# A one-layer decoder step on one core: where the last scaling's inputs and the sums of the down weights are loaded and made

## The chip, the cores and the metric

The kernel runs on one core of one Trainium2 chip, as one program. Its engines are PE (TensorE, the matmuls, with its weight loads shown as PEld), DVE (VectorE), ACT (ScalarE), POOL (GpSimd) and SP (SyncE). All transfers of this kernel are issued from SP's queue, in the order in which they stand there. The metric is the time of one execution on the device in microseconds (us), lower being better.

## The reference

One decoder layer with D_MODEL 1024 is computed in fp32 for a prompt of 2048 tokens and for 8 samples of 8 tokens each, 2112 tokens in all:

```python
def decoder_layer(x, ...):
    h = rms_norm(x, lp['pre_mix_g'])
    z = jnp.einsum('bld,de->ble', h, lp['w_in'])
    ...  # window attention, spatial gating and memory attention, each with its own gate
    x = x + rms_norm(mixed, lp['post_mix_g'])
    f, new_conv = conv_ffn(rms_norm(x, lp['pre_ffn_g']), ...)
    x = x + rms_norm(f, lp['post_ffn_g'])

def conv_ffn(h, conv_past, w_up, conv_w, conv_b, w_down):
    up = jnp.einsum('bld,df->blf', h, w_up)            # 1024 -> 2*2816
    c = conv_b; c = c + ext[:, j:j + L] * conv_w[j]    # j = 0, 1, 2, along the tokens
    act = gelu(gate) * val
    return jnp.einsum('blf,fd->bld', act, w_down)      # 2816 -> 1024
```

The change touches the second half alone: the ConvFFN and the last line, which adds the scaled result f to x. In the kernel x after the first half is called x1.

## The kernel before, in words

**Products.** An fp32 matrix is split into a rounded part and a rest (`split`: ACT casts, line 76; DVE subtracts, line 77), and a product is made of three matmuls (`PASSES`). Tokens lie along the free dimension in three groups of 704 (T2), each of two halves of 352 (CW). Big products go by Strassen's scheme: a unit has 7 products (weights a11, s1, a12, s2, s4, s3, a22), each of 12 matmuls, and the last one, a22, is run behind the first one of the next unit. In a name such as `wa11_u0_8` the letters give the weight and u0_8 group 0, unit 8. Weights a11, a12 and a22 are loaded raw (`r0`, `r1`, `r3`, line 821) and split; the sums s1 to s4 (`ws`, line 847) are loaded ready made from DRAM (`sum_d`).

**Stages.** After the first stages (to about 1560 us) comes the up projection of the ConvFFN: 3 groups of 22 units, with the convolution, gelu and product of a unit on POOL, ACT and DVE beside the matmuls (`Sink`; lines 1140 to 1183). Then follows the down projection: in each group 8 quads by the same scheme (products added into 8 tiles `ys`, lines 1229 and 1234), and a plain part for the last six blocks of 128 features (line 1279, tiles `ps_p`).

**Work inside the up projection.** Three jobs beside the units themselves are issued between units by `jobs()`. (1) `prep_sums` makes the four sums of one block of down weights: it loads 4 raw blocks, makes 4 sums on DVE (line 113), splits and stores them; there are eight such preps, d0 to d7, after every fourth unit from u0_3 to u1_11. (2) `norms` makes the row factors `rb2` of the next group from a tile of sums of squares (8 small matmuls, line 88, DVE line 92, POOL line 95, 8 small matmuls, line 98, a copy, line 1087), for each half; it is issued after unit 14. (3) `operands` loads the 8 tiles of x1 for the next group and scales each by `rb2` on DVE (line 780), then makes sums and splits of them.

**The end of a group.** `final` makes the row factors `rs` (line 1301), scales the 8 tiles of f (line 1306), adds x1 (line 1310, tile `xf`, loaded at line 1304) and stores (line 1311). For groups 0 and 1 it is held back and issued inside the next group's first quad. The last group is cut in halves, so that only its second half stands behind the last matmul; of this one every other addition is on POOL.

**What sets the order.** The order of each engine's queue is set by a scheduler before the run. Tiles come from pools, and a tile of a pool is handed out as soon as its last user is done: `wof` holds the split or summed weights (11 buffers of 4096 bytes per partition), `rawf` the raw ones and the sums in the making (5 buffers), tag `ld` of `ldf` whole activation tiles (8 buffers), tag `x` of `sd` the x1 tiles of `final` (2 buffers), `yd` the results (10).

Of the kernel before, what the change touches and what calls it, by code (L numbers as in the profile page):

```python
# [9 lines left out]
F32 = mybir.dt.float32  # L10
# [5 lines left out]
P = 128  # L16
# [7 lines left out]
T2 = 704  # L24
CW = T2 // 2
NG2 = NTOK // T2
# [719 lines left out]
def stage2(tc, I, O, br, rbc_d, x1_d, acx_d, act_d, sum_d, sg_d, gains, split, PASSES, rstd_rows, prep_sums, m_d, acm_d):  # L746
# [148 lines left out]
    for phase in (gate_phase, mix_phase, ffn_phase):  # L895
        with ExitStack() as c2:
            for n, nm in (("ps2", "ps_"), ("ps3", "pst_")):
                env[n] = c2.enter_context(
                    tc.tile_pool(name=nm + phase.__name__, bufs=1, space=PSUM, reuse_waits="tile")
                )  # L900
            phase(c2, tc, env)
# [146 lines left out]
def ffn_phase(c2, tc, env):  # L1048

    pool = env["pool"]  # L1050
    env["lp"], env["rw"], env["wo"] = (
        pool(c2, nm, n, "right") for nm, n in (("ldf", 1), ("rawf", 5), ("wof", 11))
    )
    env["op_"] = {n: pool(c2, "f" + n, 4, "right") for n in ("b11", "t1")}
    env["op_"].update({n: pool(c2, "f" + n, 4) for n in ("b21", "t2", "b22", "t3", "t4")})
    for phase in (up_phase, down_phase):
        with ExitStack() as c3:
            phase(c3, tc, env)


def up_phase(c2, tc, env):

    nc, I, O, x1_d, acx_d, act_d, sum_d, gains, pool, ps2, Strassen, rstd_rows, prep_sums, m_d, acm_d = (
        env[n] for n in (
            "nc", "I", "O", "x1_d", "acx_d", "act_d", "sum_d", "gains", "pool", "ps2", "Strassen", "rstd_rows",
            "prep_sums", "m_d", "acm_d",
        )
    )
    op_, wo, rw, lp = (env[n] for n in ("op_", "wo", "rw", "lp"))
# [8 lines left out]
    def norms(src, nm):  # L1078

        rb = lp.tile([P, T2], F32, tag="rb", name=f"rb2_{nm}", bufs=1)  # L1080
        acc = lp.tile([P, T2], F32, tag="ld", name=f"acx_{nm}", bufs=8)
        nc.sync.dma_start(out=acc, in_=src)
        for c in range(2):
            psb = env["ps3"].tile([P, 512], F32, tag="st", name=f"ps_su{nm}_{c}", bufs=1)
            cols = slice(c * CW, (c + 1) * CW)
            rstd_rows(acc[:, cols], CW, psb[:, CW:], lambda c0, w: psb[:, c0 : c0 + w], lp, f"u{nm}_{c}")
            nc.vector.tensor_copy(out=rb[:, cols], in_=psb[:, :CW])
        return rb
# [11 lines left out]
    def late(o, rs):  # L1100

        g = NG2 - 1
        m = lp.tile([P, T2], F32, tag="ld", name=f"ml_{o}", bufs=8)
        nc.sync.dma_start(out=m, in_=m_d[o])
        x = lp.tile([P, T2], F32, tag="ld", name=f"xl_{o}", bufs=8)
        nc.sync.dma_start(out=x, in_=I["xT"][:, o, g * T2 : (g + 1) * T2])
        nc.vector.scalar_tensor_tensor(
            out=m, in0=m, scalar=gains[:, 2, o : o + 1], in1=rs, op0=ALU.mult, op1=ALU.mult
        )
        nc.vector.tensor_tensor(out=m, in0=m, in1=x, op=ALU.add)  # L1110
        nc.sync.dma_start(out=x1_d[g][o], in_=m)
        if o == 0:
            nc.scalar.activation(acx, m, AF.Square)
        else:
            nc.scalar.activation(x, m, AF.Square)
            nc.vector.tensor_tensor(out=acx, in0=acx, in1=x, op=ALU.add)
        if o + 1 == KT:
            nc.sync.dma_start(out=acx_d[g], in_=acx)
# [69 lines left out]
                nc.sync.dma_start(out=dst, in_=p)  # L1188

    def jobs():  # L1190
        ops, rs = ops0, None
        for g in range(NG2):
            for f in range(NF):
                yield f"u{g}_{f}", eng.weights(I["w3"][f], sum_d[f], False, f"u{g}_{f}"), ops, Sink(g, f)
                if f % 4 == 3 and 5 * g + f // 4 < 8:
                    i = 5 * g + f // 4
                    prep_sums(rw, wo, I["w4s"][i], sum_d[NF + 12 + i], f"d{i}")
                if g == 0 and 2 <= f < 2 + KT:
                    rs = rs or norms(acm_d, "m")
                    late(f - 2, rs)  # L1200
                if f == 14 and g + 1 < NG2:
                    rb = norms(acx_d[g + 1], str(g + 1))
            if g + 1 < NG2:
                ops = eng.operands(lambda k: x1_d[g + 1][k], f"u{g + 1}", 3, rb)

    eng.run(jobs())
    nc.sync.dma_start(out=O["ncv"], in_=ncv)


def down_phase(c2, tc, env):  # L1210
# [8 lines left out]
    op_, wo, rw, lp = (env[n] for n in ("op_", "wo", "rw", "lp"))  # L1219
    yp, sp = pool(c2, "yd", 10), pool(c2, "sd", 1)  # L1220
# [74 lines left out]
    def final(g, ys, acc, cs):  # L1295
        c0, c1 = cs[0] * CW, (cs[-1] + 1) * CW
        rs = sp.tile([P, T2], F32, tag="rs", name=f"rs_d{g}_{c0}")
        for c in cs:
            psb = env["ps3"].tile([P, 512], F32, tag="st", name=f"ps_sd{g}_{c}", bufs=1)
            rstd_rows(chunk(acc, c), CW, psb[:, CW:], lambda o0, w: psb[:, o0 : o0 + w], sp, f"d{g}_{c}")  # L1300
            nc.vector.tensor_copy(out=chunk(rs, c), in_=psb[:, :CW])
        for o in range(KT):
            x = sp.tile([P, T2], F32, tag="x", name=f"xf_{g}_{o}_{c0}", bufs=2)
            nc.sync.dma_start(out=x[:, c0:c1], in_=x1_d[g][o][:, c0:c1])
            y = ys[o][:, c0:c1]
            nc.vector.scalar_tensor_tensor(  # L1306
                out=y, in0=y, scalar=gains[:, 4, o : o + 1], in1=rs[:, c0:c1], op0=ALU.mult, op1=ALU.mult
            )
            e = nc.gpsimd if o % 2 and g + 1 == NG2 and cs[-1] else nc.vector
            e.tensor_tensor(out=y, in0=y, in1=x[:, c0:c1], op=ALU.add)  # L1310
            nc.sync.dma_start(out=O["yT"][:, o, g * T2 + c0 : g * T2 + c1], in_=y)

    end = held = None
    for g in range(NG2):
        ys = []
        for b in range(NB):
            ops = eng.operands(lambda k: act_d[8 * b + k][:, g * T2 : (g + 1) * T2], f"d{g}_{b}", None, None)
            for op in range(4):
                if b == 0:
                    ys += [yp.tile([P, T2], F32, tag="y", name=f"y_{g}_{2 * op + h}") for h in range(2)]  # L1320
                i, nm = 4 * b + op, f"d{g}_{b}_{op}"
                ws = eng.weights(I["w4s"][i], sum_d[NF + 12 + i], False, nm)
                end = quad(nm, ws, ops, ys[2 * op : 2 * op + 2], b == 0, end)
                if held:
                    final(*held)
                    held = None
        acts = load_acts(g)
        acc = sp.tile([P, T2], F32, tag="acc", name=f"acc_{g}")
        if g + 1 < NG2:
            plain(g, acts, ys, (0, 1), acc, end)  # L1330
            held, end = (g, ys, acc, (0, 1)), None
        else:
            plain(g, acts, ys, (0,), acc, end)
            plain(g, acts, ys, (1,), acc, lambda: final(g, ys, acc, (0,)))
            final(g, ys, acc, (1,))
# [135 lines left out]
```

## Time and profile before

| | |
|---|---|
| time, median of 3 runs | 3004.3 us (3001.31 to 3009.29) |
| the profiled execution's own time | 3005.72 us |
| its span, first to last instruction | 3003.9 us |
| PE busy | 2876.0 us (96%) |
| DVE, ACT, POOL busy | 69%, 47%, 16% |
| granted TensorE clock, mean over the span | 0.977 |

Of the page's parts, the line of busy shares says which engine could be the bound, and the slices show where that engine is not at nine tenths. The queries that follow from it are the waits of that engine by stretch, the timeline where it waits, and windows of its busy time with the clock it was granted. In a timeline row the bracket at the end is the idle time of the engine before the instruction, and what ended it.

### The profile page before, as it was taken

How to read it: one execution, taken by the hardware profiler on the slowest of the kernel's cores; microseconds unless marked ns; L12 is line 12 of the kernel's file. 1: busy time of each engine (PE TensorE's matmuls, PEld its weight loads, DVE VectorE, ACT ScalarE, POOL GpSimd, SP SyncE). 2: the span in 40 equal slices, each digit the busy share in tenths (PEclk: the TensorE clock that was granted, in tenths of full speed). 3: DMA queues.
4: the chain of work that ended last, by engine and by line, in shares of the span. 5: the costliest groups of instructions: out<-in, count | busy, mean ns of one | idle time of the engine just before them, and what ended most of it. 6: DMA issues, size and time to landing. Idle time of an engine off the chain costs nothing. (4 is left out here: it accounts for less than half of the span.)

```text
span 3003.9 us, 52626 instructions
## 1 busy us (share of the span) xinstructions
PE 2876.0 (96%) x19340; PEld 2829.2 (94%) x19340; DVE 2064.8 (69%) x3901; ACT 1397.5 (47%) x2799; POOL 488.3 (16%) x576
## 2 busy tenths in 40 slices
PE   8999999996999999999999899999999999999996
PEld 8998999996999999999989899999999999999996
DVE  6676567888867363478798677766775667667665
ACT  5555557333555353432235355644554454343332
POOL 3221100010000000035453121311231121000000
PEclk9999999998999999999999899999999999999998
DMA  6222224787989999867669788887777778576673
GB/s 209 53 69 85 76 68 126 258 303 248 328 296 371 332 356 346 320 212 264 212 249 364 291 304 310 319 288 278 246 277 247 240 238 279 196 273 223 233 246 119
DMA packets 310946, 732.33 MB, mean 244 GB/s; under 512 B 37968, under 2 KB 90192, under 8 KB 310672
## 3 DMA queue, kind: packets, MB, share of 16 engines
q1 hardware_dynamic: 310688, 728.97, 69.9%
q8 instruction: 153, 2.51, 0.3%
q14 instruction: 105, 0.86, 0.1%
HBM read 553.55 MB, written 176.27 MB: 243 GB/s over the span
## 5 line engine op out<-in xcount | busy, mean ns | idle before, releaser
L1023 PE MATMUL ps_p<-b,w_p 128*128 128x352 f32 x1728 | 287.2, 328 | 13.3 <-DVE m L1032 8.8
L1023 PEld LDWEIGHTS ps_p<-b,w_p 128*128 128x128 f32 x1728 | 283.3, 192 | 15.1 <-issue 10.2
L1165 DVE SCALAR_TENSOR_TENSOR c<-e,k_conv_w,c 128x704 f32<-128x704 f32 (+1 forms) x264 | 251.6, 954 | 43.3 <-ACT c L1161 36.0
L882 PE MATMUL ps_xu<-ot_u,ws_u 128*128 128x352 f32 x1584 | 274.9, 322 | 0.0
L882 PEld LDWEIGHTS ps_xu<-ot_u,ws_u 128*128 128x128 f32 x1584 | 257.1, 188 | 0.0
L1036 POOL TENSOR_TENSOR m<-m,sl 128x704 f32<-128x704 f32 x48 | 101.4, 2119 | 658.0 <-DVE sl L1035 651.8
L77 DVE TENSOR_TENSOR wa_u<-r_u,wa_u 128x512 fp32r<-128x512 f32 x198 | 138.6, 703 | 48.0 <-ACT wa_u L76 43.9
L1161 ACT ACTIVATE c<-e,k_conv_b,k_conv_w 128x704 f32<-128x704 f32 (+1 forms) x132 | 129.6, 981 | 78.6 <-DVE e L1140 43.5
L882 PE MATMUL ps_xu<-ob_u,wa_u 128*128 128x352 f32 x792 | 149.0, 325 | 9.7 <-ACT wa_u L76 9.7
L1152 POOL COPY tails<-e 128x2 f32<-128x2 f32 x88 | 79.2, 900 | 470.0 <-DVE e L1140 469.6
L882 PE MATMUL ps_xg<-ot_h,ws_g 128*128 128x352 f32 x864 | 151.1, 323 | 1.7 <-ACT ws_g L76 0.8
L882 PE MATMUL ps_wu<-ob_u,wa_u 128*128 128x352 f32 x792 | 147.0, 324 | 1.1 <-DVE ob_u L77 1.1
L882 PE MATMUL ps_yu<-ot_u,ws_u 128*128 128x352 f32 x792 | 143.2, 325 | 3.8 <-DVE sl L1035 2.2
L76 ACT CAST wa_u<-r_u 128x512 fp32r<-128x512 f32 x198 | 123.1, 623 | 47.1 <-PE ps_xu L882 15.7
L882 PEld LDWEIGHTS ps_xg<-ot_h,ws_g 128*128 128x128 f32 x864 | 140.6, 188 | 2.4 <-ACT ws_g L76 1.3
L882 PEld LDWEIGHTS ps_xu<-ob_u,wa_u 128*128 128x128 f32 x792 | 131.7, 190 | 9.9 <-ACT wa_u L76 9.9
L1279 PE MATMUL ps_p<-a,wd 128*128 128x352 f32 x864 | 140.1, 323 | 0.0
L1279 PEld LDWEIGHTS ps_p<-a,wd 128*128 128x128 f32 x864 | 138.4, 188 | 0.1
L882 PE MATMUL ps_xu<-ot_u,wa_u 128*128 128x352 f32 x792 | 138.0, 323 | 0.0
L882 PE MATMUL ps_yu<-ob_u,ws_u 128*128 128x352 f32 x792 | 137.7, 323 | 0.0
L882 PEld LDWEIGHTS ps_yu<-ot_u,ws_u 128*128 128x128 f32 x792 | 130.9, 190 | 4.6 <-DVE sl L1035 2.5
L1140 DVE TENSOR_TENSOR e<-p_u,ps_wu 128x352 f32<-128x352 f32 x66 | 34.3, 519 | 145.1 <-PE ps_wu L882 140.3
(381 smaller groups left out, 6786.2 us busy)
## 6 DMA issues: line engine op xcount, KB each, us to landing
ws_u<-sum_d SPq DMA_DIRECT2D x264, 512.0 KB, 4.9
r_u<-in_w_dram SPq DMA_DIRECT2D x286, 256.0 KB, 4.7
ws_g<-sum_d SPq DMA_DIRECT2D x96, 512.0 KB, 8.5
ws_d<-sum_d SPq DMA_DIRECT2D x96, 512.0 KB, 5.1
sum_d<-ws_u SPq DMA_DIRECT2D x88, 512.0 KB, 4.2
r_g<-in_wg_dram SPq DMA_DIRECT2D x120, 256.0 KB, 5.3
r_d<-in_w4s_dram SPq DMA_DIRECT2D x104, 256.0 KB, 4.4
sg_d<-sg SPq DMA_DIRECT2D x72, 352.0 KB, 5.0
```

The costliest lines, as they stand in the source:

```text
L76: nc.scalar.copy(out=hi, in_=src)
L77: nc.vector.tensor_tensor(out=lo, in0=src, in1=_f(hi), op=ALU.subtract)
L882: nc.tensor.matmul(ps[:, :CW], lhsT=ws[w][:, a, j], rhs=ops[o][j][:, b], start=(start and n == 0), stop=(n == 3 * HK - 1), skip_group_chec ...
L1023: nc.tensor.matmul(ps[:, c, :CW], lhsT=w[:, a, 4 * oo + k], rhs=bs[k][:, b, c * CW : (c + 1) * CW], start=(i == 0), stop=(i == 11),)
L1036: nc.gpsimd.tensor_tensor(out=mx[o], in0=mx[o], in1=sg, op=ALU.add)
L1140: lambda out, part: nc.vector.tensor_tensor(out=out, in0=part(p), in1=part(q), op=ALU.add), h, c
L1152: nc.gpsimd.tensor_copy(out=tails[:, ft], in_=e[:, T2 : T2 + 2])
L1161: nc.scalar.activation(c[:, :cwid], e[:, 2:ew], AF.Identity, bias=cb[:, ft : ft + 1], scale=cw[:, ft, 2:3])
L1165: nc.vector.scalar_tensor_tensor(out=c[:, :cwid], in0=e[:, t : t + cwid], scalar=cw[:, ft, t : t + 1], in1=c[:, :cwid], op0=ALU.mult, op1= ...
L1279: nc.tensor.matmul(ps[:, :CW], lhsT=w[k // 4][:, a, k % 4], rhs=acts[k][c][:, b], start=(n == 0), stop=(n == 3 * ND - 1),)
```

## The change

Four edits are made. The pool `wof` has 10 buffers instead of 11. The preps d0 to d7 are issued after units u0_11, u0_14, u1_2, u1_5, u1_8, u1_11, u1_14 and u2_2. `norms` is issued after unit 18 instead of 14. In `final` the x1 tiles come from 4 buffers instead of 2 for the first two groups, and for the last group from the 8 buffers of tag `ld`.

```diff
--- before.py
+++ after.py
@@ -1049,7 +1049,7 @@
 
     pool = env["pool"]
     env["lp"], env["rw"], env["wo"] = (
-        pool(c2, nm, n, "right") for nm, n in (("ldf", 1), ("rawf", 5), ("wof", 11))
+        pool(c2, nm, n, "right") for nm, n in (("ldf", 1), ("rawf", 5), ("wof", 10))
     )
     env["op_"] = {n: pool(c2, "f" + n, 4, "right") for n in ("b11", "t1")}
     env["op_"].update({n: pool(c2, "f" + n, 4) for n in ("b21", "t2", "b22", "t3", "t4")})
@@ -1188,17 +1188,18 @@
                 nc.sync.dma_start(out=dst, in_=p)
 
     def jobs():
+        preps = [(g, f) for g, fs in ((0, (11, 14)), (1, (2, 5, 8, 11, 14)), (2, (2,))) for f in fs]
         ops, rs = ops0, None
         for g in range(NG2):
             for f in range(NF):
                 yield f"u{g}_{f}", eng.weights(I["w3"][f], sum_d[f], False, f"u{g}_{f}"), ops, Sink(g, f)
-                if f % 4 == 3 and 5 * g + f // 4 < 8:
-                    i = 5 * g + f // 4
+                if (g, f) in preps:
+                    i = preps.index((g, f))
                     prep_sums(rw, wo, I["w4s"][i], sum_d[NF + 12 + i], f"d{i}")
                 if g == 0 and 2 <= f < 2 + KT:
                     rs = rs or norms(acm_d, "m")
                     late(f - 2, rs)
-                if f == 14 and g + 1 < NG2:
+                if f == 18 and g + 1 < NG2:
                     rb = norms(acx_d[g + 1], str(g + 1))
             if g + 1 < NG2:
                 ops = eng.operands(lambda k: x1_d[g + 1][k], f"u{g + 1}", 3, rb)
@@ -1300,7 +1301,10 @@
             rstd_rows(chunk(acc, c), CW, psb[:, CW:], lambda o0, w: psb[:, o0 : o0 + w], sp, f"d{g}_{c}")
             nc.vector.tensor_copy(out=chunk(rs, c), in_=psb[:, :CW])
         for o in range(KT):
-            x = sp.tile([P, T2], F32, tag="x", name=f"xf_{g}_{o}_{c0}", bufs=2)
+            if g + 1 == NG2:
+                x = lp.tile([P, T2], F32, tag="ld", name=f"xf_{g}_{o}_{c0}", bufs=8)
+            else:
+                x = sp.tile([P, T2], F32, tag="x", name=f"xf_{g}_{o}_{c0}", bufs=4)
             nc.sync.dma_start(out=x[:, c0:c1], in_=x1_d[g][o][:, c0:c1])
             y = ys[o][:, c0:c1]
             nc.vector.scalar_tensor_tensor(
```

**DVE, up projection, before.** The scaling of x1 for group 1 (`x_u1`, line 780) and what stands around it; `d1` is the second prep, `u0_8` the unit whose weights come next.

```order
L780 SCALAR_TENSOR_TENSOR x_u1_0_21183<-x_u1_0_21183,c_gains_164,rb2_1_20117 128x704
L780 SCALAR_TENSOR_TENSOR x_u1_1_21189<-x_u1_1_21189,c_gains_164,rb2_1_20117 128x704
L780 SCALAR_TENSOR_TENSOR x_u1_2_21195<-x_u1_2_21195,c_gains_164,rb2_1_20117 128x704
L780 SCALAR_TENSOR_TENSOR x_u1_3_21201<-x_u1_3_21201,c_gains_164,rb2_1_20117 128x704
L780 SCALAR_TENSOR_TENSOR x_u1_4_21227<-x_u1_4_21227,c_gains_164,rb2_1_20117 128x704
L780 SCALAR_TENSOR_TENSOR x_u1_5_21233<-x_u1_5_21233,c_gains_164,rb2_1_20117 128x704
L780 SCALAR_TENSOR_TENSOR x_u1_6_21239<-x_u1_6_21239,c_gains_164,rb2_1_20117 128x704
L790 TENSOR_TENSOR t_u1_0_21207<-x_u1_0_21183 128x352
L113 TENSOR_TENSOR s3_d1_19078<-r1_d1_19076,s2_d1_19070 128x512
L790 TENSOR_TENSOR t_u1_1_21212<-x_u1_1_21189 128x352
L780 SCALAR_TENSOR_TENSOR x_u1_7_21245<-x_u1_7_21245,c_gains_164,rb2_1_20117 128x704
L790 TENSOR_TENSOR t_u1_2_21217<-x_u1_2_21195 128x352
```

**DVE, up projection, after.** The same scaling in the changed kernel.

```order
L1087 COPY rb2_1_20641<-ps_su1_1_20657 128x352
L1140 TENSOR_TENSOR e0_0_19_20693<-p1_u0_19_20708,ps_wu0_19_20747 128x352
L1179 TENSOR_TENSOR c0_0_18_20622<-c0_0_18_20622,c1_0_18_20725 128x704
L780 SCALAR_TENSOR_TENSOR x_u1_0_21087<-x_u1_0_21087,c_gains_164,rb2_1_20641 128x704
L780 SCALAR_TENSOR_TENSOR x_u1_1_21093<-x_u1_1_21093,c_gains_164,rb2_1_20641 128x704
L780 SCALAR_TENSOR_TENSOR x_u1_2_21099<-x_u1_2_21099,c_gains_164,rb2_1_20641 128x704
L780 SCALAR_TENSOR_TENSOR x_u1_3_21105<-x_u1_3_21105,c_gains_164,rb2_1_20641 128x704
L780 SCALAR_TENSOR_TENSOR x_u1_4_21131<-x_u1_4_21131,c_gains_164,rb2_1_20641 128x704
L780 SCALAR_TENSOR_TENSOR x_u1_5_21137<-x_u1_5_21137,c_gains_164,rb2_1_20641 128x704
L780 SCALAR_TENSOR_TENSOR x_u1_6_21143<-x_u1_6_21143,c_gains_164,rb2_1_20641 128x704
L780 SCALAR_TENSOR_TENSOR x_u1_7_21149<-x_u1_7_21149,c_gains_164,rb2_1_20641 128x704
L77 TENSOR_TENSOR wa22_u0_20_20827<-r3_u0_20_20828,wa22_u0_20_20827 128x512
```

The sums of prep d1 stood on both sides of the eight scalings (its fourth sum `s3_d1` behind seven of them); now no row of a prep stands near them, and what follows is a weight of unit 20.

**SP, the end of the program, before.** The last 12 rows of transfers; `xf` are loads of x1, `out_yT` stores of the result.

```order
L1311 DMA out_yT_dram<-y_2_0_31363 128x352
L1311 DMA out_yT_dram<-y_2_2_31536 128x352
L1304 DMA xf_2_3_352_33150<-x1_d2_159 128x352
L1304 DMA xf_2_4_352_33155<-x1_d2_159 128x352
L1311 DMA out_yT_dram<-y_2_3_31537 128x352
L1311 DMA out_yT_dram<-y_2_4_31655 128x352
L1304 DMA xf_2_5_352_33160<-x1_d2_159 128x352
L1304 DMA xf_2_6_352_33165<-x1_d2_159 128x352
L1311 DMA out_yT_dram<-y_2_5_31656 128x352
L1311 DMA out_yT_dram<-y_2_6_31774 128x352
L1304 DMA xf_2_7_352_33170<-x1_d2_159 128x352
L1311 DMA out_yT_dram<-y_2_7_31775 128x352
```

**SP, the end of the program, after.** Twelve of its last 18 rows; the load of `xf_2_0_352` stands some rows above.

```order
L1308 DMA xf_2_1_352_33140<-x1_d2_159 128x352
L1315 DMA out_yT_dram<-y_2_6_31774 128x352
L1315 DMA out_yT_dram<-y_2_7_31775 128x352
L1308 DMA xf_2_2_352_33145<-x1_d2_159 128x352
L1308 DMA xf_2_3_352_33150<-x1_d2_159 128x352
L1308 DMA xf_2_4_352_33155<-x1_d2_159 128x352
L1308 DMA xf_2_5_352_33160<-x1_d2_159 128x352
L1308 DMA xf_2_6_352_33165<-x1_d2_159 128x352
L1308 DMA xf_2_7_352_33170<-x1_d2_159 128x352
L1315 DMA out_yT_dram<-y_2_1_31364 128x352
L1315 DMA out_yT_dram<-y_2_3_31537 128x352
L1315 DMA out_yT_dram<-y_2_5_31656 128x352
```

The loads stood between the stores, each pair behind the stores of an earlier pair; now all eight stand ahead of `y_2_1`, the first store of this half (the two stores above it are of the half before).

**DVE, first quads of group 1 in the down projection, before.** The last rows ahead of the scaling of group 0's result (line 1306), which is 8 rows long; its first two are shown.

```order
L77 TENSOR_TENSOR wa22_d1_0_2_29953<-r3_d1_0_2_29954,wa22_d1_0_2_29953 128x512
L77 TENSOR_TENSOR wa11_d1_0_3_30054<-r0_d1_0_3_30055,wa11_d1_0_3_30054 128x512
L1301 COPY rs_d0_0_29747<-ps_sd0_1_29761 128x352
L1306 SCALAR_TENSOR_TENSOR y_0_0_27986<-y_0_0_27986,c_gains_164,rs_d0_0_29747 128x704
L1306 SCALAR_TENSOR_TENSOR y_0_1_27987<-y_0_1_27987,c_gains_164,rs_d0_0_29747 128x704
```

**DVE, the same place after**, from the last two rows of that scaling on; the copy of `rs` now stands right behind `wa22_d1_0_2`.

```order
L1310 SCALAR_TENSOR_TENSOR y_0_6_28330<-y_0_6_28330,c_gains_164,rs_d0_0_29747 128x704
L1310 SCALAR_TENSOR_TENSOR y_0_7_28331<-y_0_7_28331,c_gains_164,rs_d0_0_29747 128x704
L77 TENSOR_TENSOR wa11_d1_0_3_30054<-r0_d1_0_3_30055,wa11_d1_0_3_30054 128x512
L1314 TENSOR_TENSOR y_0_0_27986<-y_0_0_27986,xf_0_0_0_29774 128x704
L1314 TENSOR_TENSOR y_0_1_27987<-y_0_1_27987,xf_0_1_0_29779 128x704
```

The rest of weight `wa11_d1_0_3` (line 77) stood ahead of the copy of `rs`; in the changed kernel it stands behind the scaling and ahead of the first addition of `xf`.

## Rows read from the trace of the kernel before

**Rows 1.** windows: busy us by engine, granted clock, DMA share, GB/s
```profile
1690.00:1700.00 10.00, 6.05 (x19) 5.58 (x20) 7.37 (x15) 2.28 (x4) 0.00 (x0) 0.50 0.77 243
1720.00:2100.00 380.00, 380.00 (x2385) 379.75 (x2385) 270.03 (x401) 202.15 (x363) 75.55 (x114) 1.00 0.85 299
2100.00:2480.00 380.00, 380.00 (x2375) 380.00 (x2374) 261.45 (x450) 195.40 (x358) 91.72 (x198) 1.00 0.74 248
```

**Rows 2.** PE's waits, 1540 to 1720 us: total us, times, longest
```profile
PE ps_xu L882 <- ACT wa_u L76: 9.7, 1, 9.7
...
PE ps_su L98 <- POOL rstd_u L95: 2.4, 1, 2.4
...
PE ps_yu L882 <- DMA ws_u<-sum_d: 1.7, 1, 1.7
```

**Rows 3.** timeline, 1676 to 1703 us: start, duration, instruction, idle before
```profile
1677.77 0.71 PE L88 MATMUL ps_su<-ones,acx 128*88 128x1 f32 x8
...
1683.90 6.12 DVE L780 SCALAR_TENSOR_TENSOR x_u<-x_u,c_gains,rb 128x704 f32<-128x704 f32 x7
...
1684.38 7.03 SPq L821 DMA_DIRECT2D r_u<-in_w_dram  x3
...
1691.09 0.62 ACT L76 CAST ws_d<-s_d 128x512 fp32r<-128x512 f32 x1 [10.01 <-DVE s_d L113]
...
1692.28 0.95 PE L882 MATMUL ps_xu<-ob_u,wa_u 128*128 128x352 f32 x2 [9.66 <-ACT wa_u L76]
...
1695.49 3.88 PE L882 MATMUL ps_yu<-ot_u,ws_u 128*128 128x352 f32 x12 [1.67 <-DMA ws_u<-sum_d]
...
1701.88 1.28 PE L882 MATMUL ps_wu<-ob_u,wa_u 128*128 128x352 f32 x7
```

**Rows 4.** timeline, 2094 to 2108 us, the scaling for the last group
```profile
2095.58 1.02 PE L98 MATMUL ps_su<-ident,rstd_u 88*128 88x88 f32 x8
...
2098.51 2.67 DVE L780 SCALAR_TENSOR_TENSOR x_u<-x_u,c_gains,rb 128x704 f32<-128x704 f32 x3
...
2098.88 2.08 PE L882 MATMUL ps_yu<-ob_u,ws_u 128*128 128x352 f32 x12
...
2100.80 1.92 PE L882 MATMUL ps_xu<-ob_u,wa_u 128*128 128x352 f32 x11
...
2101.70 4.39 DVE L780 SCALAR_TENSOR_TENSOR x_u<-x_u,c_gains,rb 128x704 f32<-128x704 f32 x5
```

**Rows 5.** page, DMA issues: KB each, median us to landing
```profile
ws_u<-sum_d SPq DMA_DIRECT2D x264, 512.0 KB, 4.9
```

**Rows 6.** waits of PE from 2480 us to the end
```profile
PE ps_xd L882 <- ACT y L1229: 17.5, 3, 6.8
```

**Rows 7.** timeline, 2662 to 2684 us, change of group in down
```profile
2667.48 6.99 DVE L1306 SCALAR_TENSOR_TENSOR y<-y,c_gains,rs_d 128x704 f32<-128x704 f32 x8
...
2677.86 0.45 ACT L1229 COPY y<-ps_xd 128x352 f32<-128x352 f32 x1 [5.77 <-DMA out_yT_dram<-y]
```

**Rows 8.** timeline, 2960 us to the end
```profile
2961.41 4.06 DVE L1306 SCALAR_TENSOR_TENSOR y<-y,c_gains,rs_d 128x352 f32<-128x352 f32 x8
...
2976.45 0.76 PE L88 MATMUL ps_sd<-ones,acc 128*88 128x1 f32 x8 [1.99 <-DVE acc L1293]
...
2978.13 0.15 DVE L92 TENSOR_SCALAR rstd_d<-ps_sd 88x4 f32<-88x4 f32 x1
...
2982.24 4.72 DVE L1306 SCALAR_TENSOR_TENSOR y<-y,c_gains,rs_d 128x352 f32<-128x352 f32 x8
...
2983.40 1.20 POOL L1310 TENSOR_TENSOR y<-y,xf 128x352 f32<-128x352 f32 x1 [3.82 <-DVE y L1306]
...
2986.89 1.11 DVE L1310 TENSOR_TENSOR y<-y,xf 128x352 f32<-128x352 f32 x2
...
3000.25 0.92 POOL L1310 TENSOR_TENSOR y<-y,xf 128x352 f32<-128x352 f32 x1 [3.44 <-DMA xf<-x_d]
...
3001.20 0.33 SPq L1311 DMA_DIRECT2D out_yT_dram<-y  x1
```

## The prediction

> **What bounds the kernel now.** I read the page's busy shares first: PE is busy for 2876.0 of 3003.9 us, so only the stretches where PE is not busy can be won, and anything else helps only by shortening one of them. Then the windows: from 1720 to 2480 us, most of the up projection, PE is busy for all of 380.00 and of 380.00 us at the full clock [rows 1], so nothing done beside it there costs time. Then the waits of PE on both sides of that stretch. Before it there are three that belong to one place: 9.7 us on a weight's cast, 2.4 us on POOL's rstd and 1.7 us on a load of sums [rows 2]. Behind it stand 17.5 us in three waits on the copies into y [rows 6]. Last, the timeline at those places and behind the last matmul: after 2976.45 us PE has only the small matmuls of the row factor left, and the end is set by the additions of x1, each of which waits for its load [rows 8].
>
> The first place, 1677.77 to 1701.88 us, reads as follows [rows 3]. Seven scalings of x_u1 stand on DVE from 1683.90 for 6.12 us, and the fourth sum of prep d1 is ordered behind them. SP, with the raw buffers taken by that prep, needs 7.03 us for three loads of weights. ACT idles 10.01 us for the sum, and only behind the sum's cast comes the cast that PE waits for, 9.66 us. So neither the burst nor the prep is the cause alone: the burst delays the prep, the prep holds ACT's order and the buffers, and PE pays.
>
> **The change, part by part.**
>
> *The preps and the norms.* What PE did from 1677.77 to 1701.88, 24.11 us, is 16 small matmuls and 2 + 2 + 12 + 10 = 26 big ones. At the full clock 12 big ones take 1.92 us (2098.88 to 2100.80), the small ones 0.71 and 1.02 us [rows 3, 4]. So the work is worth 26 x 0.16 + 1.73 = 5.9 us and the loss is 18.2 us. Of it 2.4 + 9.7 + 1.7 are waits; the rest is mostly the clock after them, granted at 0.50 from 1690 to 1700 us [rows 1], the lower of its two levels (1.2 GHz), at which 12 matmuls took 3.88 us [rows 3]. In the new order the scaling of x_u1 has no prep beside it, and the burst by itself cost PE nothing the other time it ran: 2.67 and 4.39 us of scaling for group 2 lie inside a stretch in which PE never stopped [rows 1, 4]. Six preps (d2 to d7) lay in that stretch as well, so a prep by itself also cost nothing. I take the whole 18.2 us as gained; it would be nearer 9 if a smaller collision comes in its place, and nothing if an equal one does. The wait of 2.4 us on rstd is in the 18.2: in the new order 29 matmuls stand between the two sets of small ones, 29 x 0.16 = 4.6 us of cover for a chain of that length.
>
> *Ten weight buffers instead of eleven.* A unit uses 7 of them in 7 x 1.92 = 13.44 us. With 11, a buffer can be handed out 10 products ahead of its use, 19.2 us; with 10, 17.3 us. A load of sums lands in 4.9 us [rows 5], so between preps nothing is late. A prep holds four of them for a while and leaves 5 products, 9.6 us, where it was 11.5. That still covers 4.9, but not 4.9 plus the 7.03 us that three issues took when the raw buffers were held [rows 3], which would be 2.3 us over, at worst at each of the preps. Bounds: 0, and 8 preps x about 1.2 us (half of them that late) = 9 us. The row nearest to it is the full 760 us of PE with six preps at 11.5 us [rows 1], so I take 2 us lost. A gain I exclude: fewer buffers start no load earlier.
>
> *The last scaling.* Before, two x1 tiles are loaded at a time; behind the scaling, which starts at 2982.24, the additions run at the pace of a load, a store and a wait, to 3000.25 + 0.92 us, and the span ends 2.7 us after the last store is issued at 3001.20 [rows 8]. After, all eight loads of the last half stand ahead of its first store, and their buffers are free when the additions of the half before are done, so they land before 2981 us. Two things follow. First, the row factor: DVE's line 92 started at 2978.13, though the small matmuls were done at 2976.45 + 0.76 = 2977.21; it stood behind an addition that waited for x1. With about 0.1 us of handing over that is 0.8 us earlier, and the scaling starts at 2981.4. Second, the additions. DVE needs at least 4.06 us for eight scalings without POOL beside them, and 4 x 0.55 us for its own additions, 6.3 us. With one POOL addition beside it the scaling took 4.72, or 0.66 more [rows 8]; four such make it 8.9 us. The last store is issued at most 0.4 us later. So the end lies between 2981.4 + 6.3 + 2.7 = 2990.4 and 2981.4 + 8.9 + 0.4 + 2.7 = 2993.4, a gain of 13.5 to 10.5 us. I take 11.5, nearer the lower one, since the only scaling with POOL beside it shows the stretch.
>
> The Trainium skill, page "SBUF — State Buffer", on the shared port pair, says more against this: a VectorE instruction with two SBUF inputs and a GpSimd instruction exclude each other, and the later one waits for the whole of the other. By that rule the four additions of POOL, 0.92 us each alone [rows 8], would add 3.7 us to DVE's 6.3, and the gain would be about 9.4 to 9.8 us. The trace agrees that there is a price, but shows 0.66 us of it for one addition rather than 0.92.
>
> *Four x1 tiles for groups 0 and 1.* PE's wait there is 6.8 us at its longest and ends with ACT's copy into y, which waited 5.77 us for the first store of the old result [rows 6, 7]. That store needs the eight scalings, 6.99 us [rows 7], and one addition; its two x1 tiles were there already. More tiles cannot start it earlier. In the new order one subtraction of 0.7 us (line 77) stands between the scaling and the first addition, and the scaling starts earlier by as much, where it stood before. I take 0 for both changes together, bounds 1.5 lost and 1.5 gained (one such subtraction each way, twice).
>
> *Sum.* 3005.7 (the profiled execution) - 18.2 - 11.5 + 2 + 0 = 2978.0 us. That execution was 1.4 us over the median of the runs shown, so the forecast is 2976.6, rounded to 2977 us.
>
> **The rivals.**
>
> (a) *The collision comes back elsewhere.* In the new order the scaling for group 2 lies just ahead of prep d4, and d7 runs in the last group, where DVE has more to do per unit. For it: the chain of the first place needs only a prep and a burst whose rows meet. Against it: the burst for group 2 now has a weight of the next unit between its second and third scaling, and no sum behind it waits on PE's next product. It gives back between half and all of 18.2: 2986 to 2995 us.
>
> (b) *The end shortens by half.* The eight stores and the additions on two engines could be limited by the queue rather than by the loads. For it: all go by one queue, and the span ends 2.7 us after the issue of the last store, so each store takes about that long. Against it: the addition that came last names a load as what it waited for, not a store [rows 8]. With 5.5 us instead of 11.5: 2983 us.
>
> (c) *Slower: ten buffers are too few.* If a weight load often took more than the 17.3 us that the ring now gives it, PE would wait in each of the 66 units and 24 quads. At 0.5 us a time that is 45 us, against 30 gained: 3020 us. It decides from 0.33 us a unit. For it: the DMA engines are busy 0.85 and 0.74 of the time in the up projection [rows 1], and loads queue behind each other. Against it: 4.9 us of landing is far from 17.3.
>
> (d) *The loads don't come earlier.* The buffers of tag `ld` also hold the activations of the last six blocks; were they freed late, the loads would wait behind them. The new order of SP has the loads ahead of the stores, which speaks against it. Then only the first gain stays: 2988 us.
>
> **How the numbers follow.** The forecast gets 0.68, (a) 0.13, (b) 0.10, (c) 0.05, (d) 0.04. The forecast's own range is 2970 to 2984: the end's bounds of 1 and 2 us, the ring's 0 and 9, the group changes' 1.5 each way, and some 4 us between runs of one kernel. To 8 in 10 it takes in (b) and the lower part of (a): 2969 to 2992 us. A measurement of this kernel tells about 0.3%, 9 us, from no change. Faster by more than that means under 2995 us: the forecast, (b), (d), nearly all of (a), less a reserve of 0.04 for a mechanism not seen: 0.90. Slower is (c) with a little of that reserve, 0.05; the same is left with 0.05.
>
> **What would show it.** Right: no wait of PE over 2 us between 1600 and 1720 us and a granted clock of 1.00 there; the scaling of x_u1 some 11 units later with PE busy through it; behind the last matmul additions one after the other with no wait for x1, and 11 to 12 us instead of 21.7 from the start of the last scaling to the end; the two waits of about 6.8 us at the group changes still there. Wrong: new waits of PE on loads of ws_u or on casts of wa_u near the preps, above all at u2_2 and u2_3, or additions that still wait for loads of x1. A time over 2992 us would say that the first place was paid for again; one under 2969 that the group changes shortened too.

## The result, and the profile after

The changed kernel takes 2983.62 us (median of 5 runs, 2978.49 to 2990.12) against 3004.3 us: a ratio of 0.9934, 95% interval 0.9915 to 0.9952, so 14 to 26 us faster. Forecast were 2977 us, within 2969 to 2992. The profiled execution took 2983.34 us, its span is 2981.6 us.

The two profiles differ by 5.2 us before the first `ps_yu` product, the second product of the up projection (1565.84 and 1560.64 us). In the twelve profiles of this study it starts between 1559.7 and 1566.2 us, so I compare stretches behind that point: up, from there to the last `ps_yu` product of the up units; down, from there to the last eight small matmuls of line 88; end, the rest of the span. They are good to about 0.1 us.

| | up | down | end | sum |
|---|---|---|---|---|
| before, us | 911.5 | 499.1 | 27.5 | 1438.1 |
| after, us | 893.9 | 510.2 | 16.9 | 1421.0 |
| difference | -17.6 | +11.1 | -10.6 | -17.1 |

Two stretches came out nearly as forecast; the one in the middle lost 11 us. The stretches together give 17.1 us and the medians 20.7; the interval of 14 to 26 us holds both.

**Up.** PE's waits of [rows 2] are gone: no wait of PE is listed from 1600 to 2450 us, where the forecast had allowed 2 us for ten buffers. First two windows of the changed kernel (columns as in [rows 1]); the clock in the place of the stall is 1.00:

```profile
1560.60:1720.00 159.40, 157.68 (x997) 157.04 (x998) 119.81 (x181) 87.84 (x158) 36.58 (x51) 1.00 0.85 313
1720.00:2450.00 730.00, 730.00 (x4581) 729.98 (x4580) 521.29 (x840) 387.90 (x687) 168.95 (x304) 1.00 0.81 284
```

Then the timeline of the changed kernel where the eight scalings of `x_u1` stand now, some 11 units later:

```profile
1830.69 2.08 PE L882 MATMUL ps_yu<-ob_u,ws_u 128*128 128x352 f32 x12
...
1831.17 6.98 DVE L780 SCALAR_TENSOR_TENSOR x_u<-x_u,c_gains,rb 128x704 f32<-128x704 f32 x8
...
1832.61 1.92 PE L882 MATMUL ps_xu<-ob_u,wa_u 128*128 128x352 f32 x11
...
1834.37 2.08 PE L882 MATMUL ps_xu<-ot_u,ws_u 128*128 128x352 f32 x12
```

The scalings take as long as before (6.98 us for eight, 6.12 for seven [rows 3]), but PE goes on, 1.92 us a product.

**End.** Timeline of the changed kernel from 2964 us, which answers to [rows 8]:

```profile
2964.74 0.76 PE L88 MATMUL ps_sd<-ones,acc 128*88 128x1 f32 x8 [2.23 <-DVE acc L1294]
2965.60 0.16 DVE L92 TENSOR_SCALAR rstd_d<-ps_sd 88x4 f32<-88x4 f32 x1 [1.01 <-PE ps_sd L88]
...
2969.50 6.07 DVE L1310 SCALAR_TENSOR_TENSOR y<-y,c_gains,rs_d 128x352 f32<-128x352 f32 x8
2970.72 1.15 POOL L1314 TENSOR_TENSOR y<-y,xf 128x352 f32<-128x352 f32 x1 [3.88 <-DVE y L1310]
2971.89 7.11 SPq L1315 DMA_DIRECT2D out_yT_dram<-y  x8
2972.32 1.20 POOL L1314 TENSOR_TENSOR y<-y,xf 128x352 f32<-128x352 f32 x1 [0.46 <-DVE y L1310]
2973.99 1.20 POOL L1314 TENSOR_TENSOR y<-y,xf 128x352 f32<-128x352 f32 x1 [0.46 <-DVE y L1310]
2975.49 2.55 DVE L1314 TENSOR_TENSOR y<-y,xf 128x352 f32<-128x352 f32 x4
```

No addition waits for x1. Line 92 follows the small matmuls at once, and from the start of the scaling to the end of the span it is 12.1 us instead of 21.7. The scaling took 6.07 us: 4.06 and three times 0.67 for the three additions of POOL beside it, which is the stretch of 0.66 read from one addition.

**Down.** The waits of PE in the changed kernel from 2470 us on (columns as in [rows 2]):

```profile
PE ps_xd L882 <- DVE wa_d L77: 11.6, 3, 5.3
PE ps_xd L882 <- ACT y L1230: 8.4, 4, 3.6
PE ps_sd L88 <- DVE acc L1294: 2.2, 1, 2.2
PE ps_xd L882 <- ACT wa_d L76: 1.7, 1, 1.7
```

Against 17.5 us in three waits [rows 6] there are now 21.7 us in eight, and more of them are followed by the lower clock. Two places have to be told apart. The first is a change of group, which answers to [rows 7]:

```profile
2650.82 6.99 DVE L1310 SCALAR_TENSOR_TENSOR y<-y,c_gains,rs_d 128x704 f32<-128x704 f32 x8
...
2657.73 0.68 DVE L77 TENSOR_TENSOR wa_d<-r_d,wa_d 128x512 fp32r<-128x512 f32 x1
...
2658.47 3.30 PE L882 MATMUL ps_xd<-ob_d,wa_d 128*128 128x352 f32 x10 [5.32 <-DVE wa_d L77]
...
2663.87 0.45 ACT L1230 COPY y<-ps_xd 128x352 f32<-128x352 f32 x1 [2.46 <-DMA out_yT_dram<-y]
...
2664.38 3.14 PE L882 MATMUL ps_xd<-ot_d,ws_d 128*128 128x352 f32 x12 [2.61 <-ACT y L1230]
```

PE now stops twice: for the rest of `wa11_d1_0_3`, behind the eight scalings, and then still for the stores of old results. Both times the lower clock follows: the granted clock is 0.50 from 2658.47 to 2661.80 us and 0.65 on average from 2664.38 to 2667.50, and 10 matmuls take 3.30 us, 12 take 3.14; at the full clock 12 take 1.92 [rows 4]. Waits and the time that the slow rows take over the full clock come to 11.2 us at the first change and 10.4 at the second, against 8.2 and 9.2 before: 4.2 us lost. The second place is the start of the down projection:

```profile
2471.84 0.59 PE L882 MATMUL ps_xd<-ob_d,wa_d 128*128 128x352 f32 x2 [1.66 <-ACT wa_d L76]
...
2473.38 2.67 PE L882 MATMUL ps_xd<-ob_d,wa_d 128*128 128x352 f32 x10 [0.94 <-DVE wa_d L77]
...
2477.10 3.89 PE L882 MATMUL ps_xd<-ot_d,ws_d 128*128 128x352 f32 x12 [1.06 <-ACT y L1230]
...
2479.73 0.33 SPq L1188 DMA_DIRECT2D act_d<-e  x1
...
2486.84 0.45 ACT L1230 COPY y<-ps_yd 128x352 f32<-128x352 f32 x1 [9.09 <-DMA act_d<-e]
...
2488.06 4.11 PE L882 MATMUL ps_xd<-ot_d,ws_d 128*128 128x352 f32 x15 [3.64 <-ACT y L1230]
```

Before, PE stopped once here, 3.9 us and 2.4 us of lower clock behind it:

```profile
2498.80 3.89 PE L882 MATMUL ps_xd<-ot_d,ws_d 128*128 128x352 f32 x12 [3.86 <-ACT y L1229]
```

Now there is another wait, which ends with ACT's copy into a result tile, and that copy waited 9.09 us for the store of the last unit's activations. Waits and lower clock together are 12.0 us against 6.3: 5.7 lost.

### The profile page after: what moved, and what is told of

Its sections match the earlier page's. It is cut to its first block, busy times and chain, and to the rows that moved or that the text cites. A ratio compares the mean times of both kernels' runs of the same rounds, so it can differ in the third digit from the quotient of the medians.

```text
span 2981.6 us, 52598 instructions
## 1 busy us (share of the span) xinstructions
PE 2871.4 (96%) x19340; PEld 2823.4 (95%) x19340; DVE 2059.5 (69%) x3901; ACT 1403.2 (47%) x2799; POOL 487.7 (16%) x576
## 4 chain that ended last, share of the span: by engine, by line
PE 83%; DMA 6%; DVE 6%; ACT 2%; issue 1%; POOL 1%; SPq 0%; DVEq 0%; ACTq 0%; POOLq 0%
PE ps_xu L882 17%; PE ps_xg L882 9%; PE ps_yu L882 8%; PE ps_p L1023 8%; PE ps_xd L882 6%; PE ps_yg L882 5%; PE ps_p L1280 5%; PE ps_wu L882 4%; PE ps_q L215 3%; PE ps_yd L882 3%; PE ps_mqp L229 3%; PE ps_wg L882 2%; PE ps_kv L215 2%; DMA r_u<-in_w_dram 1%; PE ps_wd L882 1%
## 5 line engine op out<-in xcount | busy, mean ns | idle before, releaser
L882 PEld LDWEIGHTS ps_wu<-ob_u,wa_u 128*128 128x128 f32 x792 | 130.7, 188 | 1.4 <-DVE ob_u L77 1.4
```

Source lines behind the costliest of these rows:

```text
L882: nc.tensor.matmul(ps[:, :CW], lhsT=ws[w][:, a, j], rhs=ops[o][j][:, b], start=(start and n == 0), stop=(n == 3 * HK - 1), skip_group_chec ...
```

## The experiments

My theory after the result: the up and end gains belong to the moved preps and to the eight tiles; the loss in down belongs to the ten buffers. Rivals are named with each run. The table has all runs. A ratio is to runs of the kernel before made together with that run (their medians are 3004.1, 3005.3 and 3002.6 us); up, down and end are from the profiles, as above.

| kernel | median us | ratio (95%) | up | down | end |
|---|---|---|---|---|---|
| e1_tail | 2995.45 | 0.9972 (0.9960 to 0.9983) | 911.6 | 498.8 | 16.8 |
| e2_preps_norms | 2993.55 | 0.9963 (0.9949 to 0.9977) | 893.4 | 507.8 | 27.0 |
| e3_both_no_buf | 2980.96 | 0.9924 (0.9910 to 0.9937) | 893.4 | 506.8 | 16.8 |
| e7_wof10 | 3012.90 | 1.0029 (1.0020 to 1.0038) | 914.9 | 504.5 | 26.6 |
| e5_preps | 2990.96 | 0.9954 (0.9938 to 0.9969) | 892.8 | 505.7 | 27.2 |
| e6_norms | 3011.61 | 1.0029 (1.0017 to 1.0041) | 911.2 | 508.1 | 27.5 |
| e8_after_x2 | 2987.19 | 0.9938 (0.9926 to 0.9951) | 893.1 | 508.4 | 17.1 |
| e10_swap | 2975.33 | 0.9899 (0.9886 to 0.9913) | 893.2 | 499.9 | 16.4 |
| e11_after_swap | 2985.45 | 0.9941 (0.9929 to 0.9954) | 893.7 | 510.4 | 16.7 |
| c9_swap_y12 | 2959.73 | 0.9848 (0.9835 to 0.9862) | 893.8 | 485.9 | 16.6 |

**e1_tail**, the last group's loads alone:

```diff
-            x = sp.tile([P, T2], F32, tag="x", ..., bufs=2)
+            x = lp.tile(..., tag="ld", bufs=8) if g + 1 == NG2 else sp.tile(..., tag="x", bufs=2)
```

> Of the four edits only one is made: in the last group the x1 tiles of the last scaling come from the 8 buffers of tag ld (11 weight buffers, 2 x1 tiles in the other groups, preps and norms as before). My theory: this edit is worth what the end showed, 10.6 us from the start of the last eight small matmuls of line 88 to the end of the span (16.9 instead of 27.5 us), so 2993 to 2995 us, ratio about 0.9965; the stall at unit u0_8 and the waits of 6.8 us at the group changes are unchanged. Rival: the end is faster only because the queue and the scheduler had more room after the other edits; then the gain is under 6 us.

Measured 2995.45 us, 8.7 us less than before and 0.5 us above the range. In the profile the end is 16.8 us, as said, and up and down stay within 0.3 us. The edit alone brings the whole 10.7 us of the end.

**e2_preps_norms**, the two moves alone:

```diff
+        preps = [(g, f) for g, fs in ((0, (11, 14)), (1, (2, 5, 8, 11, 14)), (2, (2,))) for f in fs]
...
-                if f % 4 == 3 and 5 * g + f // 4 < 8:
+                if (g, f) in preps:
...
-                if f == 14 and g + 1 < NG2:
+                if f == 18 and g + 1 < NG2:
```

> Only the places of the preps and of the norms are changed (11 weight buffers, x1 tiles and end as before). My theory: the collision at u0_8 goes, worth 18.2 us, and nothing else moves: about 2986 us, ratio about 0.994, waits at the change from up to down and at the group changes as in the kernel before (3.9, 6.8, 6.8 us). Rival: the later preps are what cost 5.7 us at the change from up to down in the changed kernel; then that loss is here too and the gain is 12 to 13 us, 2991 us.

Up is 18.1 us shorter, as said, but the median only 10.6 us lower: the rival was right about down, which lost 8.7 us with eleven buffers, some 7 of them at its start. The new wait there comes with the moves.

**e3_both_no_buf**, the changed kernel with `("wof", 11)` and `bufs=2` again:

```diff
-        ... ("wof", 10)
+        ... ("wof", 11)
-                x = sp.tile(..., tag="x", bufs=4)
+                x = sp.tile(..., tag="x", bufs=2)
```

> The changed kernel without its two edits of buffers: 11 weight buffers again, 2 x1 tiles in groups 0 and 1, everything else as changed. My theory: the ten weight buffers are what costs about 10 us in the down projection (5.7 at its start, 4.2 at the two group changes), so this gains both parts whole, 18.2 + 10.6 = 28.8 us: about 2975 us, ratio 0.990, and the profile shows waits of 6.8 us on ACT y at the group changes and none on DVE wa_d. Rival: the losses came with the preps or with the x1 loads of the last group; then the time is that of the changed kernel, 2982 to 2984 us.

2980.96 us, between theory and rival. Eleven buffers win back the waits on `wa_d` (none is left), but the start of down still has its second wait. Its timeline:

```profile
2482.66 0.33 SPq L1188 DMA_DIRECT2D act_d<-e  x1
...
2489.53 0.45 ACT L1230 COPY y<-ps_xd 128x352 f32<-128x352 f32 x1 [9.93 <-DMA act_d<-e]
```

**e7_wof10**, ten buffers alone:

```diff
-        ... ("wof", 11)
+        ... ("wof", 10)
```

> Only the pool of weights is changed, 10 buffers instead of 11. My theory: the scheduler puts the rest of weight wa11 of the fourth quad behind the eight scalings at each group change, PE waits about 5.3 us for it and then still for ACT y, and the start of the down projection has further waits: 8 to 10 us slower than before, 3012 to 3014 us, ratio 1.003; the up projection gets new waits near the stall of u0_8 at most. Rival: four x1 tiles are behind the losses (their pool lies where other tiles lay); then this kernel is like before, within 3 us.

8.8 us slower, as said, but by another sum: down is 5.4 us longer and up 3.4, where the stall grew to 15.7 us, which was not expected in that size. Its waits of PE in down are those on `wa_d`, without the long one on the store:

```profile
PE ps_xd L882 <- DVE wa_d L77: 11.6, 3, 5.3
PE ps_xd L882 <- ACT y L1229: 3.2, 3, 1.2
```

So the ten buffers and the moves cost down separately. My theory held for the group changes alone: the start of down loses nothing with ten buffers and the old places.

**Where the second wait comes from.** The result tiles of down lie in SBUF where tiles of the up projection lay, and a copy into one waits until the old tile is done. The order of SP around the last store of activations is the same in e2_preps_norms as before; what differs is the place of the tile that this store reads, `e0_2_21`, one of six equal buffers that are handed out as they come free. The addresses in the built programs, with the wait of PE that goes back to this store:

```
kernel           result tiles over e0_2_21   wait of PE on ACT y, us
before, e1, e7   y_0_5, y_0_6                none
after, e8        y_0_3, y_0_4                3.6, 4.5
e2, e3, e5       y_0_2, y_0_3                3.3, 4.1, 4.4
e6               y_0_1, y_0_2                6.9
e11              y_0_0                       7.6
e10, c9          y_0_7, none                 none
```

In each of these programs but c9, where no tile of the first group lies there, the copy into the first of the tiles named waits for the semaphore count that this very store makes up. Where that tile is among the first two that are needed, PE waits 6.9 and 7.6 us, with the next two 3.3 to 4.5, and later not at all. Three runs were made to test this.

**e10_swap**, e3_both_no_buf with the two pools of down laid out the other way round:

```diff
-    yp, sp = pool(c2, "yd", 10), pool(c2, "sd", 1)
+    sp, yp = pool(c2, "sd", 1), pool(c2, "yd", 10)
```

> The kernel of e3_both_no_buf with one line changed: in the down projection the pool of small tiles (sd) is laid out in SBUF ahead of the pool of results (yd), so that the first result tiles y_0_1 to y_0_4 lie where no tile of the last up units lay. My theory: the wait of PE on ACT y 9 us after the start of the down projection (3.3 to 4.1 us, and 2.4 to 2.9 us of the lower clock behind it) comes from y_0_2 or y_0_3 lying over e0_2_21, the tile that the last store of activations reads; it goes, and the 3.9 us at the start go too, where y_0_1 lay over e1_2_21: 6 to 12 us less than e3_both_no_buf, 2969 to 2975 us. Rival: the wait comes from the store or from the queue itself, which now carries the preps later; then 2981 us as e3_both_no_buf.

5.6 us less than e3_both_no_buf, just short of the range: the second wait is gone, the first one shrank to 2.8 us instead of going. `y_0_0` lies over `e0_2_20` here, and its copy waits for that tile's store. The waits of PE from 2450 to 2700 us (the 6.8 us are a change of group):

```profile
PE ps_xd L882 <- ACT y L1230: 9.6, 2, 6.8
```

**e6_norms**, the place of the norms alone, 18 for 14:

```diff
-                if f == 14 and g + 1 < NG2:
+                if f == 18 and g + 1 < NG2:
```

> Only the norms are moved, from after unit 14 to after unit 18 (preps, buffers and end as before). In the order of DVE the scaling of x1 for group 1 still stands at unit 8 beside the fourth sum of d1. My theory of the stall: it is the prep's meeting with the scaling, so the wait of 9.7 us on wa_u stays. My theory of the start of the down projection: e0_2_21, which the last store reads, now lies under y_0_1 and y_0_2, earlier than in any kernel so far, so the wait comes with the first quad: one wait of 9 us or more on ACT y, with the lower clock behind it, instead of 3.9. Together 5 to 9 us slower than before, 3009 to 3013 us. Rival: the norms are what removed the stall; then the up projection is 18 us shorter and the time under 2995 us.

9.0 us slower than before. The stall stays, and the wait for the store is 6.9 us; it came in addition to the 3.9 us, not in place of it. The longest waits of PE from 1600 us on:

```profile
PE ps_xd L882 <- ACT y L1229: 17.5, 3, 6.8
PE ps_xu L882 <- ACT wa_u L76: 9.7, 1, 9.7
PE ps_yd L882 <- ACT y L1229: 6.9, 1, 6.9
```

**e11_after_swap**, the same swap in the changed kernel:

```diff
-    yp, sp = pool(c2, "yd", 10), pool(c2, "sd", 1)
+    sp, yp = pool(c2, "sd", 1), pool(c2, "yd", 10)
```

> The changed kernel with the pool of small tiles laid out ahead of the pool of results, as in e10_swap, and nothing else (10 weight buffers and 4 x1 tiles stay). My theory: the first result tiles no longer lie over e0_2_21, so the wait of 3.6 us and the lower clock behind it go, 5 to 7 us: 2976 to 2979 us; what is left over e10_swap (2975.3 us) is the price of ten weight buffers at the two group changes, about 4 us. Rival: with ten buffers the weights set the pace at the start and nothing is gained: 2982 to 2985 us.

A miss: 2985.45 us, nothing is gained. I had taken over the addresses of e10_swap; with four x1 tiles the pool of small tiles, which now lies ahead, is longer, and `y_0_0`, needed first of all, falls on `e0_2_21`. PE waits 7.6 us for the copy into it. The trace puts the end of that copy's wait down to a load of raw weights, but the count that the copy waits for is the one made up by the store of `e0_2_21`. So the miss speaks for the cause and against my forecast.

**e5_preps**, the preps moved, the norms not:

```diff
-                if f % 4 == 3 and 5 * g + f // 4 < 8:
+                if (g, f) in preps:
```

> Only the preps are moved; the norms stay after unit 14, so the scaling of x1 for group 1 stays about unit 8 but no prep stands beside it (11 weight buffers, old end). My theory: the burst alone costs PE nothing, so there is no wait over 1 us from 1600 to 1720 us and the up projection is as short as in e2_preps_norms, 18 us less than before; e0_2_21 again lies under y_0_2 and y_0_3, so about 6 us are lost at the start of the down projection: 2991 to 2994 us. Rival: the burst itself stalls the split of unit 8's weights and 5 us or more of the wait stay: 2998 us or more.

2990.96 us is at the lower end of what was said, and up is 892.8 us, so the move of the preps is the whole gain in up. But the premise was wrong: the scaling did not stay at unit 8, it went to 1775.84 us, some 7 units later (in the changed kernel it stands at 1831 us). Its eight scalings are one burst there, no prep stands beside them, and PE is busy throughout. A timeline row and a window (columns as in [rows 1]):

```profile
1775.84 6.99 DVE L780 SCALAR_TENSOR_TENSOR x_u<-x_u,c_gains,rb 128x704 f32<-128x704 f32 x8
...
1760.00:1800.00 40.00, 40.00 (x261) 40.00 (x260) 33.23 (x52) 17.44 (x31) 12.69 (x13) 1.00 0.84 297
```

So the burst alone costs PE nothing at unit 15. At unit 8 without a prep it was not seen.

**e8_after_x2**, the changed kernel with two x1 tiles:

```diff
-                x = sp.tile(..., tag="x", bufs=4)
+                x = sp.tile(..., tag="x", bufs=2)
```

> The changed kernel with 2 x1 tiles in groups 0 and 1 instead of 4 (10 weight buffers, preps, norms and the last group's loads as changed). My theory: more x1 tiles don't bring the first store of a group forward, and the waits at the group changes come from the ten weight buffers: the time is that of the changed kernel, 2981 to 2986 us, with 5.3 us on DVE wa_d at each group change. Rival: the four tiles already pay for part of what the ten buffers cost; then this is 4 us or more slower, 2988 us.

2987.19 us, between theory and rival; its interval overlaps that of the changed kernel. Down is 508.4 against 510.2 us in the profiles, with the same 5.3 us on `wa_d` twice. Whether four tiles bring anything can't be told.

**c9_swap_y12**, e10_swap with other sizes:

```diff
-    sp, yp = pool(c2, "sd", 1), pool(c2, "yd", 10)
+    sp, yp = pool(c2, "sd", 1), pool(c2, "yd", 12)
-                x = sp.tile(..., tag="x", bufs=2)
+                x = sp.tile(..., tag="x", bufs=1)
```

> As e10_swap, and with 12 result tiles instead of 10 and one x1 tile instead of two in groups 0 and 1 (their bytes pay for it). My theory: the second quad of a new group no longer needs a tile of the old one, so the waits of 6.8 and 7.1 us and the lower clock behind them (1.6 and 2.4 us) go: about 18 us less than e10_swap, 2951 to 2957 us. Rival: with a single x1 tile the stores come one per load and addition, some 4.5 us each, and the third and fourth quads wait for them instead: 2965 us or more.

2959.73 us, about 45 us under the kernel before and 24 under the changed one, the fastest of all, though 2.7 us above the range. The two new sizes were not run apart. The waits of PE from 2440 us on have none of 6.8 us:

```profile
PE ps_xd L882 <- ACT y L1230: 6.5, 2, 6.0
PE ps_sd L88 <- DVE acc L1294: 2.2, 1, 2.2
PE ps_wd L882 <- ACT wa_d L76: 1.4, 2, 0.7
```

15.6 us came off e10_swap, not 18: the wait at the start of down grew from 2.8 to 6.0 us. `y_0_0` now lies over `c0_2_21`, a tile of the last unit, and its copy waits for line 1185, which reads that tile:

```profile
2476.61 0.45 ACT L1230 COPY y<-ps_xd 128x352 f32<-128x352 f32 x1 [4.89 <-DVE e L1185]
```

## Why the prediction was right, and where not

The time lies in the range, but 6.6 us above the forecast. It falls on the 2983 us of rival (b), though not by (b)'s way: the end gained 10.6 us and not 5.5. Of (a), (c) and (d) nothing shows, since PE has no wait from 1600 to 2450 us and no addition of the end waits for x1. That two places in down which the sum had at nothing cost 9.9 us and the time still lies in the range is in part luck: the range was made wide for the rivals.

**The stall of 18.2 us** was sized rightly. 17.6 to 18.7 us went in every kernel with moved preps, and the stall stayed in e1, e6 and e7. That the burst and the prep are needed together is supported by e5, where the burst alone costs nothing at unit 15, but was not shown at unit 8. That the norms had to move too was not shown: e5 gains as much without.

**Ten buffers, 2 us lost in up:** with the preps moved, up is within 0.5 us with ten and with eleven buffers (893.9 and 893.4 us), and no wait is listed. The price came elsewhere.

**The end, 11.5 us** (10.5 to 13.5): 10.6. The terms held one by one: line 92 earlier, 0.66 for a POOL addition beside the scaling, about 2.6 us behind the last store.

**The group changes, 0 with bounds of 1.5 us,** is the step that failed. I read in the order that `wa11` moves behind the scaling, and priced it as 0.7 us on DVE, the length of one subtraction. Its price is that of the wait of its user: PE needs this weight for the next product, and the eight scalings, 7.0 us, now stand ahead of it. The wait on ACT y behind it became shorter as PE came later (2.6 and 1.1 us instead of 6.8), which kept the loss to 4.2 us. So the sign that I had named, the two waits of about 6.8 us still there, did not come. e3 and e7 put this loss down to the ten buffers.

**The start of the down projection** was no term of the sum. The 3.9 us there stand among the 17.5 us of [rows 6], and I took the place as unchanged because its order is. It lost 5.7 us through an address. With both, and without the 2 us for ten buffers, the forecast's own sum for the profiled execution would have been 2978.0 - 2 + 9.9 = 2986 us; the 5.2 us by which the stages ahead of the change happened to differ make it 2981, where 2983.3 was measured. The rest is spread over all three stretches (0.6 us in up, 0.9 in the end, 1.2 in down) and was not followed up.

By the rule of the Trainium skill's page "SBUF — State Buffer", section "Who interferes with whom", under which a VectorE instruction with two SBUF inputs and a GpSimd instruction that reads SBUF contend and the later one is blocked, three additions of 0.92 us would cost the scaling 2.8 us, as an estimate. The runs show 2.0 us, 0.67 for each of the three beside the scaling, and POOL's additions take 1.15 to 1.20 us there instead of 0.92: a price for both engines, and for DVE less than the whole of POOL's additions.

Not settled: why the scheduler pulled the scaling to unit 8 in the first place, why up lost 3.4 us with ten buffers and the old preps, and what would remain of the wait at the start of down if no early result tile lay over tiles of the last two units (no such layout was run).

## What to carry to other kernels

Where an instruction moves behind a long row of others on its engine, charge the wait of whoever uses its result, not its own length. Two phases that share memory are tied by addresses as well as by order: look up which tiles the first outputs of the next phase lie over, and who still reads those. And a smaller pool has to be checked at every place that uses it, not only where it is tightest.

## What the runs showed that I had not expected

The kernel with ten buffers alone (e7_wof10) shows no wait of PE in up after 1700 us, so behind none of the preps d2 to d7, and a ring that covers 17 us by the prediction's count was enough for loads that land in 4.9; yet with it an edit of memory alone made the stall of unit 8 grow from 9.7 to 15.7 us. And two lines that only say where pools lie and how many tiles they have (e3_both_no_buf to c9_swap_y12) were worth 21 us, about as much as the change under study.
